# Dealing light expert groups at 0.92 instead of 0.86, and putting the routing weights behind the routing sort

## The chip, the cores and the metric

The kernel runs on one core of a Trainium2 chip. The metric is the device time of one execution in microseconds (us). Before the change it is 2007.69 us, the median of 3 runs (2006.3 to 2009.74).

## The reference

The program is a stack of two blocks over 256 tokens of width 1024, in float32: two hybrid layers (a gated recurrence beside dilated attention, then an MLP), a pooling mixer with a SwiGLU, and an attention mixer followed by a mixture of experts. Only the last part is touched:

```python
def moe_ffn(x, router, w_gu, w_down):
    B, S, D = x.shape
    xt = x.reshape(B * S, D)
    logits = (xt @ router).astype(jnp.float32)
    top_v, top_i = lax.top_k(logits, TOP_K)
    w = jax.nn.softmax(top_v, axis=-1)
    combine = jnp.einsum('tk,tke->te', w, jax.nn.one_hot(top_i, N_EXPERTS, dtype=jnp.float32)).astype(x.dtype)
    y = jnp.zeros_like(xt)
    for e in range(N_EXPERTS):
        y = y + combine[:, e:e + 1] * swiglu(xt, w_gu[e], w_down[e])
    return y.reshape(B, S, D)
```

Each expert has 1024 x 7168 gate and up weights and 3584 x 1024 down weights, so the eight experts read some 352 MB of weights, which is most of what the mixture does. A layer norm of `ALPHA * x + y` ends the program.

## The kernel before, in words

**Routing.** `Route.choose` ranks the logits of each token, `Route.place` counts the tokens of each expert, and `route_order` (L1193 on) sorts the experts by their count, heaviest first, with one-hot matrices on VectorE (DVE): `sort` (L1210 to L1214) multiplies the one-hot matrix `ge` with a column of `Q` and sums. Column 0 gives the experts' numbers, which are written to `ri` (L1218), from which the SP queue reads which expert's weights to load. Columns 2 and 3 give each token's slot, from which `select` (L1279) makes the matrices `P` that gather the tokens. Column 1 and `ov` (L1222 to L1224) say whether an expert has more tokens than the kernel's sizes allow, which leads to a branch at the end (L1635). Lines 1225 to 1246 make the weights of the choice: the two logits of each token, a softmax of two, and its sorted form `cw`. The program's scheduler orders the instructions of each engine; `high_priority` moves the sorts of columns 0, 2 and 3 to the front, and `behind(K, [i])` issues what is in it after instruction `i`.

**Experts.** The experts in sorted order are `E[0]` to `E[7]`. `E[0]` has two tiles of tokens (128 and 64 rows), `E[1]` to `E[3]` one of 128, `E[4]` and `E[5]` one of 64, `E[6]` and `E[7]` one of 32. Each expert is cut into 7 steps f of 512 hidden columns, and each step into 3 groups: gate (`up1`), up (`up2`) and down. A group reads 2 MB of weights in two blocks of 1 MB (`wload`, L132, tile `raw`, 7 buffers). `run_experts` is a generator that yields once a group.

- A group of `E[0]` to `E[3]` is split: ScalarE (ACT) rounds a block to `whi` (L147), DVE writes the rest to `wlo` (L148; 4 buffers of each), and TensorE (PE) multiplies three times (L209 to L211), 24 matmuls of 512 columns a group for a tile of 128 tokens. These experts are called heavy here.
- A group of `E[4]` to `E[7]` is not split: PE reads `raw` itself (L1340). The order lists 8 such matmuls a group, and the trace has two records for each. These experts are called light.

In `moe_layer` the heavy generator runs, and after each of its groups a number `due` grows; as many light groups as `due` says are dealt out between the heavy ones, in the order `E[6], E[7], E[4], E[5]`. What is left over comes after the heavy experts. The last down step of the last heavy expert is `finish`, which loads its weights in smaller parts. The sums over an expert's down steps stay in PSUM, for the second tile of `E[0]` in `sacc`; `weigh` (L1497, L1498) scales the sum of an expert by its weights, and `combine` (L1511 to L1513) adds it to `y`. After the branch at L1635 comes the layer norm (L283 to L291) and the store.

```python
            light, done, due = go([E[6], E[7], E[4], E[5]]), 0, 0.0
            for e, f in go(E[:4], hook, True):
                if E[6].tiles[0].xg is not None:
                    due += 0.86 if e.p else 1.5
                while done < int(due) and next(light, None):
                    done += 1
            for _ in light:
                pass
```

Of the kernel before, what the change touches and what calls it, by code (L numbers as in the profile page):

```python
# [13 lines left out]
AF = mybir.ActivationFunctionType  # L14
OP = mybir.AluOpType
AX = mybir.AxisListType
# [96 lines left out]
def wide(pool, n, size, dt=F32, **kw):  # L113


    return pool.tile([128, size // 4], dt, **kw)[:, :n]


def bc(ap, n):

    return ap[..., None].to_broadcast(list(ap.shape) + [n])
# [30 lines left out]
def behind(K, hold=None):  # L152

    es = ExitStack()
    for ins in K.hold if hold is None else hold:
        es.enter_context(K.tc.issue_after(ins.ins))
    return es
# [56 lines left out]
def bank(K, tag):  # L214
    return K.ps.tile([128, 512], F32, name=tag, tag=tag, bufs=K.banks[tag])
# [974 lines left out]
def route_order(K, pool, S):  # L1190


    nc = K.nc  # L1193
    sc, Q, lg, cst = S.sc, S.Q, S.lg, S.cst
    cnt = Q[:, 1, :]
    ca = cnt[:, :, None].to_broadcast([128, 8, 8])
    cb = cnt[:, None, :].to_broadcast([128, 8, 8])
    gt, ge = sc(8, 8), sc(8, 8)
    nc.vector.tensor_tensor(gt, cb, ca, op=OP.is_gt)
    nc.vector.tensor_tensor(ge, cb, ca, op=OP.is_equal)  # L1200
    nc.vector.tensor_tensor(ge, ge, cst("tri").rearrange("p (a b) -> p a b", a=8), op=OP.mult)
    nc.vector.tensor_tensor(gt, gt, ge, op=OP.add)
    pos = sc(8)
    nc.vector.tensor_reduce(pos, gt, axis=AX.X, op=OP.add)
    nc.vector.tensor_tensor(ge, pos[:, None, :].to_broadcast([128, 8, 8]),
                            cst("i8p").rearrange("p (a b) -> p a b", a=8), op=OP.is_equal)
    R = wide(pool, 48, 192 + 64, name="R").rearrange("p (a b) -> p a b", a=6)
    ri = pool.tile([1, 17], I32, name="ri")

    def sort(*qs):  # L1210
        for q in qs:
            g = sc(8, 8)
            nc.vector.tensor_tensor(g, ge, Q[:, q:q + 1, :].to_broadcast([128, 8, 8]), op=OP.mult)
            nc.vector.tensor_reduce(R[:, q, :], g, axis=AX.X, op=OP.add)  # L1214

    with K.tc.high_priority():
        sort(0)
        nc.vector.tensor_copy(ri[:, 0:8], R[0:1, 0, :])  # L1218
        sort(2, 3)
    sort(1)  # L1220
    ov = sc(9)[0:1]
    nc.vector.tensor_tensor(ov[:, 0:8], R[0:1, 1, :], cst("lim")[0:1, :], op=OP.is_gt)  # L1222
    nc.vector.tensor_reduce(ov[:, 8:9], ov[:, 0:8], axis=AX.X, op=OP.max)
    nc.vector.tensor_copy(ri[:, 16:17], ov[:, 8:9])  # L1224
    f = sc(2, 2, 8)
    for r in range(2):
        nc.vector.tensor_scalar(f[:, r], S.rk, float(r), None, op0=OP.is_equal)
    top = sc(2, 2, 8)
    sm = sc(6, 2)
    for r in range(2):  # L1230
        nc.vector.tensor_tensor(top[:, r], f[:, r], lg, op=OP.mult)
        nc.vector.tensor_reduce(sm[:, r, :], top[:, r], axis=AX.X, op=OP.add)
    nc.vector.tensor_tensor(sm[:, 2, :], sm[:, 1, :], sm[:, 0, :], op=OP.subtract)
    nc.scalar.activation(sm[:, 2, :], sm[:, 2, :], AF.Exp)
    nc.vector.tensor_scalar(sm[:, 3, :], sm[:, 2, :], 1.0, None, op0=OP.add)
    nc.vector.reciprocal(sm[:, 3, :], sm[:, 3, :])
    nc.vector.tensor_tensor(sm[:, 4, :], sm[:, 2, :], sm[:, 3, :], op=OP.mult)

    nc.vector.tensor_tensor(Q[:, 4:6, :], f[:, 0], bc(sm[:, 3, :], 8), op=OP.mult)
    nc.vector.tensor_tensor(top[:, 0], f[:, 1], bc(sm[:, 4, :], 8), op=OP.mult)  # L1240
    nc.vector.tensor_tensor(Q[:, 4:6, :], Q[:, 4:6, :], top[:, 0], op=OP.add)
    sort(4, 5)
    cw = pool.tile([128, 8, 2, 2], F32R, name="cw")
    for t in range(2):
        nc.vector.tensor_copy(cw[:, :, t, 0], R[:, 4 + t, :])
        nc.vector.tensor_tensor(cw[:, :, t, 1], R[:, 4 + t, :], cw[:, :, t, 0].bitcast(F32), op=OP.subtract)
    return R, ri, cw
# [315 lines left out]
def moe_layer(K, x, A, out, ps1, S):  # L1563
    nc = K.nc
    with ExitStack() as es:
# [6 lines left out]
        with K.tc.tile_pool(name="exp", reuse_waits="tile", bufs=1) as ep:  # L1572
            ps1.close()
            K.ps = es.enter_context(K.tc.tile_pool(name="psx", reuse_waits="tile", bufs=1,
                                                   space=bass.MemoryType.PSUM))
            K.banks = {"mm": 4, "acc": 4}
            K.iota = S.cst("iota")
            E = [Expert(p, t) for p, t in enumerate(([F0, H(128)], [F0], [F0], [F0], [(0, "s")], [(0, "s")], [(0, "q")],
                                                     [(0, "q")]))]
            with behind(K, [K.beat(5, S.last)]):  # L1580
                K.beat(14, S.place(1))
            R, ri, cw = route_order(K, pool, S)
            nc.vector.tensor_copy(K.identr, K.ident)
            K.iota = K.xp.tile([128, 256], F32, name="iota", tag="junk")[:, :128]
            nc.vector.tensor_copy(K.iota, S.cst("iota"))
            y = K.xTp.tile([128, 2, D], F32, name="y", tag="xT0")
            ye = K.xTp.tile([128, 2, D], F32R, name="ye", tag="xT1")
            K.ye, K.weighed = (ye[:, 0], ye[:, 1]), None
            for t in range(2):
                nc.vector.tensor_scalar(y[:, t, :], x[:, t, :], ALPHA, None, op0=OP.mult)  # L1590
            go = lambda *a: run_experts(K, ep, A, x, R, ri, cw, y, *a)
            E[0].tiles[1].sb = True
            b = [ep.tile([128, 2048], t, name=f"box{n}") for n, t in enumerate((F32R, F32, F32))]
            K.boxes["xg1"] = [b[0][:, 0:1024].rearrange("p (k o m) -> p k o m", o=1, m=128)]
            K.boxes["hT1"] = [b[0][:, c:c + 512].rearrange("p (k o m) -> p k o m", o=1, m=128) for c in (1024, 1536)]
            K.boxes["sg1"], K.boxes["sacc"] = [b[1][:, c:c + 512] for c in (0, 512)], [b[1][:, 1024:2048]]
            K.boxes["sgl"] = [b[2][:, c:c + 512] for c in (1024, 1536)]
            few_xg = b[2][:, 0:1024].rearrange("p (k m) -> p k m", m=128), ep.tile([128, KT, 64], F32, name="xgq")

            def few(xg, *ps):  # L1600

                w = xg.shape[2]
                P = ep.tile([128, 2, 128], F32, name="PL")[:, :, :w]
                for c, p in enumerate(ps):
                    tl = E[p].tiles[0]
                    o = slice(c * tl.m, (c + 1) * tl.m)
                    select(K, ep, R, p, tl)
                    for t in range(2):
                        nc.vector.tensor_copy(P[:, t, o], tl.P[:, t, :tl.m])
                    gather_w(K, ep, cw, p, tl, f"l{p}")  # L1610
                    tl.xg = xg[:, :, o]
                for k0 in range(0, KT, 4):
                    g = bank(K, "mm")[:, :4 * w].rearrange("p (a b) -> p a b", a=4)
                    for k in range(k0, k0 + 4):
                        for t in range(2):
                            nc.tensor.matmul(g[:, k % 4, :], x[:, t, k * 128:(k + 1) * 128], P[:, t, :],
                                             start=t == 0, stop=t == 1)
                    nc.scalar.activation(xg[:, k0:k0 + 4, :], g, AF.Copy)

            def hook(i):  # L1620
                if i == 0:
                    few(few_xg[1], 6, 7)
                if i == 2:
                    few(few_xg[0], 4, 5)

            light, done, due = go([E[6], E[7], E[4], E[5]]), 0, 0.0
            for e, f in go(E[:4], hook, True):
                if E[6].tiles[0].xg is not None:
                    due += 0.86 if e.p else 1.5
                while done < int(due) and next(light, None):  # L1630
                    done += 1
            for _ in light:
                pass
            over = nc.values_load(ri[0:1, 16:17], min_val=0, max_val=1)
            with K.tc.If(over > 0):  # L1635
                K.line = []
                rest = ((0, H(192)), (1, F1), (2, F1), (4, H(64)), (5, H(64)), (6, H(32)), (7, H(32)))
                for _ in go([Expert(p, [t]) for p, t in rest]):
                    pass
        with K.tc.tile_pool(name="fin", reuse_waits="tile", bufs=1) as fp:  # L1640
            g = row_bc(K, fp, A["ln_g_2"][1, 1], D, "lng")
# [123 lines left out]
```

## Time and profile before

| what | value |
|---|---|
| median of 3 runs | 2007.69 us (2006.3 to 2009.74) |
| the profiled execution, its own time | 2002.88 us |
| its span, first to last instruction | 2001.1 us |
| granted TensorE clock, mean | 0.989 |
| PE busy | 97% of the span |
| DVE busy | 63% |
| ACT busy | 48% |
| HBM read | 520.73 MB |

The span is the time between the first and the last instruction that the profile shows; 1.8 us of the execution lie around it. The profiled execution is 4.8 us below the median of the runs. The mixture of experts takes the stretch from about 1082 to 1987 us of the span. In the views, an engine's busy time is the union of its instructions' times; PEld is TensorE's loading of stationary operands, which runs beside its matmuls. An entry in square brackets is the idle time of that engine just before the row, with what ended it.

### The profile page before, as it was taken

The page shows a single profiled execution, that of the slowest core. Times are in us where ns is not written, and L with a number is a line of the kernel's source. Part 1 is how long each engine was busy: PE and PEld are TensorE (multiplying, and loading weights), DVE is VectorE, ACT ScalarE, POOL GpSimd, SP SyncE. Part 2 cuts the span into 40 slices and gives each one's busy share as a digit, 9 for nine tenths or more (in the row PEclk, how much of TensorE's full clock was granted, in tenths as well). Part 3 has the DMA queues.
Part 4 walks back from the last instruction along what each step waited for, and adds up shares of the span by engine and source line. Part 5 has one row for each costly group of instructions (what it writes and reads, how often), then busy time and mean ns, then how long its engine had stood idle before and what let it go on. Part 6 is the DMA issues. An engine that isn't in the chain of part 4 may idle for free. (4 is left out here: it accounts for less than half of the span.)

```text
span 2001.1 us, 27902 instructions
## 1 busy us (share of the span) xinstructions
PE 1934.3 (97%) x11066; PEld 1488.1 (74%) x11066; DVE 1263.4 (63%) x1723; ACT 960.8 (48%) x1197; POOL 33.5 (2%) x39
## 2 busy tenths in 40 slices
PE   7999999999999899999999999999999999999996
PEld 7879998887999899989877766666556655655563
DVE  6876555886556654466767655666765665656655
ACT  6565444665444433434343554445554554454442
POOL 0000000000000200000000000000000000000000
PEclk9999999999999999999998999999999999999998
DMA  9434554534555355551103989999999999999994
GB/s 345 164 115 158 180 191 168 183 129 169 194 185 189 137 202 188 173 195 53 48 1 144 371 365 381 389 400 368 426 427 419 403 397 417 405 406 380 419 419 167
DMA packets 137851, 523.68 MB, mean 262 GB/s; under 512 B 12016, under 2 KB 44144, under 8 KB 94832
## 3 DMA queue, kind: packets, MB, share of 16 engines
q1 hardware_dynamic: 137568, 521.74, 67.4%
q8 instruction: 89, 1.46, 0.3%
q14 instruction: 50, 0.41, 0.1%
q10 hardware_dynamic: 144, 0.07, 0.0%
HBM read 520.73 MB, written 1.05 MB: 261 GB/s over the span
## 5 line engine op out<-in xcount | busy, mean ns | idle before, releaser
L148 DVE TENSOR_TENSOR wlo<-raw,whi 128x2048 fp32r<-128x2048 f32 (+2 forms) x335 | 715.7, 2155 | 318.3 <-ACT whi L147 310.1
L147 ACT ACTIVATE whi<-raw 128x2048 fp32r<-128x2048 f32 (+2 forms) x337 | 600.2, 1805 | 307.3 <-issue 69.3
L209 PE MATMUL mm<-xT,whi 128*128 128x256 f32 (+1 forms) x824 | 237.2, 288 | 0.8 <-ACT mqk L459 0.4
L211 PE MATMUL mm<-xT,wlo 128*128 128x256 f32 (+1 forms) x824 | 234.4, 284 | 0.0
L210 PE MATMUL mm<-xT,whi 128*128 128x256 f32 (+1 forms) x824 | 233.9, 284 | 0.3
L210 PE MATMUL acc<-wlo,hT 128*128 128x512 f32 x568 | 224.5, 395 | 5.4 <-DVE wlo L148 5.4
L211 PE MATMUL acc<-whi,hT 128*128 128x512 f32 x568 | 221.6, 391 | 0.0
L209 PE MATMUL acc<-whi,hT 128*128 128x512 f32 x568 | 216.0, 394 | 3.5 <-ACT whi L147 3.5
L209 PE MATMUL mm<-whi,xg 128*128 128x512 f32 x448 | 181.6, 405 | 4.9 <-ACT whi L147 3.2
L210 PE MATMUL mm<-wlo,xg 128*128 128x512 f32 x448 | 179.5, 401 | 4.2 <-DVE wlo L148 4.2
L211 PE MATMUL mm<-whi,xg 128*128 128x512 f32 x448 | 176.5, 394 | 0.0
L209 PEld LDWEIGHTS mm<-xT,whi 128*128 128x128 f32 (+1 forms) x824 | 156.0, 189 | 4.6 <-issue 1.1
L210 PEld LDWEIGHTS mm<-xT,whi 128*128 128x128 f32 (+1 forms) x824 | 156.0, 189 | 3.3 <-DVE xT L678 1.1
L211 PEld LDWEIGHTS mm<-xT,wlo 128*128 128x128 f32 (+1 forms) x824 | 155.9, 189 | 0.6
L210 PEld LDWEIGHTS acc<-wlo,hT 128*128 128x128 f32 x568 | 106.7, 188 | 41.2 <-DVE wlo L148 8.8
L209 PEld LDWEIGHTS acc<-whi,hT 128*128 128x128 f32 x568 | 105.9, 188 | 34.4 <-issue 8.3
L211 PEld LDWEIGHTS acc<-whi,hT 128*128 128x128 f32 x568 | 106.6, 188 | 23.5 <-issue 1.7
L209 PEld LDWEIGHTS mm<-whi,xg 128*128 128x128 f32 x448 | 84.4, 188 | 47.0 <-issue 18.8
L210 PE MATMUL mx<-xT,whi 128*128 128x256 f32 x416 | 117.7, 283 | 0.0
L211 PE MATMUL mx<-xT,wlo 128*128 128x256 f32 x416 | 117.7, 283 | 0.0
L209 PE MATMUL mx<-xT,whi 128*128 128x256 f32 x416 | 117.7, 283 | 0.0
L210 PEld LDWEIGHTS mm<-wlo,xg 128*128 128x128 f32 x448 | 84.6, 189 | 36.9 <-issue 12.3
(381 smaller groups left out, 2902.3 us busy)
## 6 DMA issues: line engine op xcount, KB each, us to landing
raw<-in_moe_gu_dram SPq DMA_DIRECT2D x224, 1024.0 KB, 9.0
raw<-in_moe_dn_dram SPq DMA_DIRECT2D x110, 1024.0 KB, 8.6
raw<-in_w_up_dram SPq DMA_DIRECT2D x32, 1024.0 KB, 5.3
raw<-in_w_down_dram SPq DMA_DIRECT2D x32, 1024.0 KB, 5.1
raw<-in_w_in_dram SPq DMA_DIRECT2D x26, 1024.0 KB, 6.0
raw<-in_ffn_w_gu_dram SPq DMA_DIRECT2D x22, 1024.0 KB, 5.0
raw<-in_ffn_w_down_dram SPq DMA_DIRECT2D x11, 1024.0 KB, 4.7
raw<-in_nsa_w_in_dram SPq DMA_DIRECT2D x10, 1024.0 KB, 4.9
```

Source lines behind the costliest of these rows:

```text
L147: nc.scalar.activation(h, d, AF.Copy)
L148: K.lo.tensor_tensor(l, d, h.bitcast(F32), op=OP.subtract)
L209: nc.tensor.matmul(ps, l[0], r[0], start=start, stop=False)
L210: nc.tensor.matmul(ps, l[0], r[1], start=False, stop=False)
L211: nc.tensor.matmul(ps, l[1], r[0], start=False, stop=stop)
```

## The change

Two things change. The constant by which light groups are dealt behind the groups of `E[1]` to `E[3]` goes from 0.86 to 0.92. And everything in `route_order` that comes after the sort of columns 0, 2 and 3, which is the check for too many tokens and the weights of the choice, is put under `behind(K, [slots])`, where `slots` is the last reduction of the sort of column 3.

```diff
-            nc.vector.tensor_reduce(R[:, q, :], g, axis=AX.X, op=OP.add)
+            last = nc.vector.tensor_reduce(R[:, q, :], g, axis=AX.X, op=OP.add)
+        return last
...
-        sort(2, 3)
-    sort(1)
-    ov = sc(9)[0:1]
...
-    f = sc(2, 2, 8)
...
-    nc.scalar.activation(sm[:, 2, :], sm[:, 2, :], AF.Exp)
...
-    sort(4, 5)
+        slots = sort(2, 3)
+    with behind(K, [slots]):
+        sort(1)
+        ov = sc(9)[0:1]
...
+        f = sc(2, 2, 8)
...
+        nc.scalar.activation(sm[:, 2, :], sm[:, 2, :], AF.Exp)
...
+        sort(4, 5)
...
-                    due += 0.86 if e.p else 1.5
+                    due += 0.92 if e.p else 1.5
```

The new program's line numbers are two higher behind the first part. The order of DVE in the sort, before (L1227 to L1241 are the weights of the choice, L1199 to L1218 the sort up to `ri`, L1279 the gather matrices):

```order
L1200 TENSOR_TENSOR route<-route 128x64
L1233 TENSOR_TENSOR route<-route 128x2
L1201 TENSOR_TENSOR route<-route 128x64
L1202 TENSOR_TENSOR route<-route 128x64
L1235 TENSOR_SCALAR route<-route 128x2
...
L1213 TENSOR_TENSOR route<-route 128x64 x4
L1240 TENSOR_TENSOR route<-route 128x16
L1214 TENSOR_REDUCE R<-route 128x8 x4
L1241 TENSOR_TENSOR route<-route 128x16
L1218 CAST ri<-R 1x8
L1279 TENSOR_SCALAR P<-iota,R 128x128 x4
```

The same place in the changed program:

```order
L1201 TENSOR_TENSOR route<-route 128x64
L1202 TENSOR_TENSOR route<-route 128x64
L1204 TENSOR_REDUCE route<-route 128x8
L1205 TENSOR_TENSOR route<-route 128x64
L1213 TENSOR_TENSOR route<-route 128x64 x3
L1214 TENSOR_REDUCE R<-route 128x8 x3
L1213 TENSOR_TENSOR route<-route 128x64
L1219 CAST ri<-R 1x8
L1229 TENSOR_SCALAR route<-route 128x16 x2
L1281 TENSOR_SCALAR P<-iota,R 128x128 x3
L1214 TENSOR_REDUCE R<-route 128x8
L1281 TENSOR_SCALAR P<-iota,R 128x128
```

The weights' instructions have left the sort; two of them (L1229) now stand between `ri` and the gather matrices, and the others behind.

The end of DVE's order before the branch, before the change, in which `hT` is the transposed operand of the last heavy step, 128x1024 and 128x512 are the parts of `finish`, and the second L1498 with its L1513 belongs to the last light expert:

```order
L225 TENSOR_TENSOR hT_15516<-mm,hT_15516 128x4x128
L148 TENSOR_TENSOR wlo<-raw,whi 128x2048
...
L1439 COPY hTl<-mm 128x256
L148 TENSOR_TENSOR wlo<-raw,whi 128x1024 x2
L148 TENSOR_TENSOR wlo<-raw,whi 128x512 x4
L1498 SCALAR_TENSOR_TENSOR ye<-acc,cs,ye 128x512 x2
L1513 TENSOR_TENSOR y<-mm,y 128x512 x4
L1498 SCALAR_TENSOR_TENSOR ye<-acc,cs,ye 128x512 x2
L1513 TENSOR_TENSOR y<-mm,y 128x512 x4
```

The same place in the changed program, from the product of the last heavy gate and up (`sg`) on:

```order
L1429 TENSOR_TENSOR sg_15439<-mm,sg_15439 128x512
L148 TENSOR_TENSOR wlo<-raw,whi 128x2048
L1500 SCALAR_TENSOR_TENSOR ye<-acc,cs,ye 128x512
L148 TENSOR_TENSOR wlo<-raw,whi 128x2048
L1500 SCALAR_TENSOR_TENSOR ye<-acc,cs,ye 128x512
...
L148 TENSOR_TENSOR wlo<-raw,whi 128x1024 x2
L225 TENSOR_TENSOR hT_15567<-mm,hT_15567 128x4x128
L148 TENSOR_TENSOR wlo<-raw,whi 128x512 x4
L1500 SCALAR_TENSOR_TENSOR ye<-acc,cs,ye 128x512
L1515 TENSOR_TENSOR y<-mm,y 128x512
L1500 SCALAR_TENSOR_TENSOR ye<-acc,cs,ye 128x512
L1515 TENSOR_TENSOR y<-mm,y 128x512 x3
```

The last light expert's L1500 and L1515 now stand ahead of the parts of `finish`, among the last whole blocks, and the heavy expert's own stand last; `hT` stands behind four whole blocks and the two parts of 1024 columns.

## Rows read from the trace of the kernel before

**Rows 1.** Busy time of each engine by stretch: mixture by stages, then one saturated stretch

```profile
core 0: us, PE busy (x) PEld busy (x) DVE busy (x) ACT busy (x) POOL busy (x), PEclk, DMA share, GB/s
1342.00:1522.00 180.00, 170.65 (x860) 107.67 (x859) 125.09 (x109) 96.09 (x86) 0.00 (x0) 0.99 0.99 410
1522.00:1942.00 420.00, 416.50 (x1837) 248.47 (x1838) 258.75 (x191) 206.54 (x165) 0.00 (x0) 1.00 0.99 406
...
1402.00:1422.00 20.00, 19.92 (x107) 11.90 (x105) 14.74 (x15) 9.83 (x13) 0.00 (x0) 1.00 1.01 426
```

**Rows 2.** Who waited for whom: SP's queue from 1082 us, PE from 1342 to 1522

```profile
SPq L132 <- PE mm L1340: 260.4, 76, 10.9
...
PE acc L209 <- ACT whi L147: 2.9, 2, 2.1
PE mm L210 <- DVE wlo L148: 2.3, 2, 1.8
PE acc L210 <- DVE wlo L148: 2.2, 2, 1.4
```

**Rows 3.** PE in order of time: heavy matmuls, then a run of light ones

```profile
1936.40 0.39 PE L211 MATMUL mm<-whi,xg 128*128 128x512 f32 x1
...
1940.48 0.39 PE L211 MATMUL mm<-whi,xg 128*128 128x512 f32 x1
1940.80 1.94 PE L1340 MATMUL mm<-raw,box 128*64 128x512 f32 x8
1942.67 0.50 PE L209 MATMUL mm<-whi,xg 128*128 128x512 f32 x1
```

**Rows 4.** Groups by line and shape in the mixture (1082 to 1990 us), PE and DVE

```profile
L1340 PE MATMUL mm<-raw,xgq 128*32 128x512 f32 x448 | 56.4, 601 | 0.4 <-DMA raw<-in_moe_gu_dram 0.4
L1340 PE MATMUL acc<-raw,hTl 128*32 128x512 f32 x224 | 29.4, 604 | 0.0
L148 DVE TENSOR_TENSOR wlo<-raw,whi 128x2048 fp32r<-128x2048 f32 x166 | 377.1, 2285 | 108.2 <-ACT whi L147 100.3 <-PE mm L1332 7.0
```

**Rows 5.** Busy time of the light matmuls (L1340) alone, from 1522 to 1942

```profile
1522.00:1942.00 420.00, 140.72 (x606) 36.41 (x608) 1.00 0.99 406
```

**Rows 6.** DVE and SP's queue in order of time: the sort

```profile
1079.55 0.62 DVE L1213 TENSOR_TENSOR route<-route 128x64 f32<-128x64 f32 x4
1080.10 0.17 DVE L1240 TENSOR_TENSOR route<-route 128x16 f32<-128x16 f32 x1
1080.18 0.59 DVE L1214 TENSOR_REDUCE R<-route 128x8 f32<-128x64 f32 x4
1080.69 0.16 DVE L1241 TENSOR_TENSOR route<-route 128x16 f32<-128x16 f32 x1
1080.77 0.15 DVE L1218 CAST ri<-R 1x8 int32<-1x8 f32 x1
...
1082.03 18.11 SPq L132 DMA_DIRECT2D raw<-in_moe_gu_dram  x11
```

**Rows 7.** PE in order of time: the first heavy matmul

```profile
1088.93 0.50 PE L209 MATMUL mm<-whi,xg 128*128 128x512 f32 x1 [2.14 <-ACT whi L147]
```

**Rows 8.** The end, in order of time: PE, then ACT, then DVE

```profile
1954.65 0.73 PE L209 MATMUL acc<-whi,hT 128*128 128x512 f32 x2 [0.62 <-ACT whi L147]
1956.98 0.50 PE L210 MATMUL acc<-wlo,hT 128*128 128x512 f32 x1 [1.59 <-DVE wlo L148]
...
1979.90 1.94 PE L1340 MATMUL acc<-raw,hTl 128*64 128x512 f32 x8
...
1952.20 0.60 ACT L224 ACTIVATE hT<-mm 128x512 fp32r<-128x512 f32 x1 [4.05 <-PE acc L211]
...
1976.09 0.69 ACT L1497 ACTIVATE ye<-acc,cs 128x512 fp32r<-128x512 f32 x1 [1.80 <-PE acc L211]
...
1976.81 0.75 DVE L1498 SCALAR_TENSOR_TENSOR ye<-acc,cs,ye 128x512 fp32r<-128x512 f32 x1 [1.74 <-ACT ye L1497]
...
1983.94 2.58 DVE L1513 TENSOR_TENSOR y<-mm,y 128x512 f32<-128x512 f32 x4
```

More of the change, by code (lines that the diff above doesn't have):

```diff
@@ L1218, in route_order @@
         nc.vector.tensor_copy(ri[:, 0:8], R[0:1, 0, :])
-        sort(2, 3)
-    sort(1)
-    ov = sc(9)[0:1]
-    nc.vector.tensor_tensor(ov[:, 0:8], R[0:1, 1, :], cst("lim")[0:1, :], op=OP.is_gt)
-    nc.vector.tensor_reduce(ov[:, 8:9], ov[:, 0:8], axis=AX.X, op=OP.max)
-    nc.vector.tensor_copy(ri[:, 16:17], ov[:, 8:9])
-    f = sc(2, 2, 8)
[L1226 to L1232, printed above, removed]
@@ L1233, in route_order @@
-    nc.vector.tensor_tensor(sm[:, 2, :], sm[:, 1, :], sm[:, 0, :], op=OP.subtract)
-    nc.scalar.activation(sm[:, 2, :], sm[:, 2, :], AF.Exp)
[L1235 to L1240, printed above, removed]
@@ L1241, in route_order @@
-    nc.vector.tensor_tensor(Q[:, 4:6, :], Q[:, 4:6, :], top[:, 0], op=OP.add)
-    sort(4, 5)
+        slots = sort(2, 3)
+    with behind(K, [slots]):
+        sort(1)
+        ov = sc(9)[0:1]
+        nc.vector.tensor_tensor(ov[:, 0:8], R[0:1, 1, :], cst("lim")[0:1, :], op=OP.is_gt)
+        nc.vector.tensor_reduce(ov[:, 8:9], ov[:, 0:8], axis=AX.X, op=OP.max)
+        nc.vector.tensor_copy(ri[:, 16:17], ov[:, 8:9])
+        f = sc(2, 2, 8)
+        for r in range(2):
+            nc.vector.tensor_scalar(f[:, r], S.rk, float(r), None, op0=OP.is_equal)
+        top = sc(2, 2, 8)
+        sm = sc(6, 2)
+        for r in range(2):
+            nc.vector.tensor_tensor(top[:, r], f[:, r], lg, op=OP.mult)
+            nc.vector.tensor_reduce(sm[:, r, :], top[:, r], axis=AX.X, op=OP.add)
+        nc.vector.tensor_tensor(sm[:, 2, :], sm[:, 1, :], sm[:, 0, :], op=OP.subtract)
+        nc.scalar.activation(sm[:, 2, :], sm[:, 2, :], AF.Exp)
+        nc.vector.tensor_scalar(sm[:, 3, :], sm[:, 2, :], 1.0, None, op0=OP.add)
+        nc.vector.reciprocal(sm[:, 3, :], sm[:, 3, :])
+        nc.vector.tensor_tensor(sm[:, 4, :], sm[:, 2, :], sm[:, 3, :], op=OP.mult)
+        nc.vector.tensor_tensor(Q[:, 4:6, :], f[:, 0], bc(sm[:, 3, :], 8), op=OP.mult)
+        nc.vector.tensor_tensor(top[:, 0], f[:, 1], bc(sm[:, 4, :], 8), op=OP.mult)
+        nc.vector.tensor_tensor(Q[:, 4:6, :], Q[:, 4:6, :], top[:, 0], op=OP.add)
+        sort(4, 5)
```

## The prediction

> **What bounds the kernel now.** I read the busy time by stretch first. The sort and the start of the experts lie at 1070 to 1090 us, and the constant acts on everything after the first heavy expert, so these are the places. From 1342 to 1522 us, where the light experts with 32 tokens stand beside `E[1]`, PE is idle for 180 - 170.65 = 9.35 us, and the transfers run at up to 426 GB/s; from 1522 to 1942, with the light experts of 64 tokens, PE is idle for only 3.5 us in 420, and the transfers fall to 406 [rows 1]. Second, the waits: SP's queue waited 260.4 us for light matmuls to free a `raw` buffer [rows 2], so over much of the mixture the transfers follow PE and not the other way round. Third, PE in order of time: heavy matmuls start every (1940.48 - 1936.40)/18 = 0.227 us without a gap [rows 3]. So the first stretch is bound by transfers, the second by PE; a light group dealt earlier costs nothing in the second, something in the first, and changes what is left for the end. Last, the end [rows 8]: after PE's last light matmuls there is a chain of ACT, DVE, PE and DVE up to the last addition to `y`, and then the branch and the layer norm, which the change does not touch.
>
> **Prices of a group.** A heavy group of 24 matmuls takes 24 x 0.227 = 5.44 us of PE; with its share of the transposes (four in three groups, an estimate of 0.22 us from the matmuls' interval, of which the full 4 x 0.227/3 would be 0.3) 5.66. The light groups from 1522 to 1942 have 606 records [rows 5], 16 a group, so 37.9 groups, which at 0.86 stand beside 44.0 heavy ones; PE's 416.5 busy us less 44.0 x 5.66 leave 4.4 us for a light group of 64 tokens with all that goes with it, of which 140.72/37.9 = 3.7 are its matmuls, and 0.7 are around them. A light group of 32 tokens has (56.4 + 29.4)/42 = 2.0 us of matmuls [rows 4]; with the same 0.7 it takes 2.7. The transfer of a group is 2.1 MB, at 426 GB/s 4.92 us [rows 1].
>
> **Part 1, the sort.** On DVE the weights' instructions stand in the gaps of a dependent chain, so most of them cost the sort nothing. What does not fit: L1240 starts at 1080.10 and the reductions at 1080.18; L1241 takes 1080.69 to 1080.77, where `ri` is written [rows 6]. That is 0.08 + 0.08; the fourth reduction now stands behind `ri`, another 0.14 (a quarter of 0.59). I take 0.3 us, between 0 and 0.5, by which the first transfer (1082.03) starts earlier. The gather matrices gain less, as two small instructions stand ahead of them now. The weights themselves come later, some twenty small instructions behind the gather matrices, at 0.62/4 = 0.155 us each [rows 6] about 3 us. The first users of `cw` are matmuls that sit in front of the first heavy one on PE; PE is idle there for 2.14 us until ACT has split the first block [rows 7], and this idle time is what hides it. If all 3 us reached PE, 3 - 2.14 = 0.9 would be left, and nothing hides that; I put +1 us into the range for it. Part 1: **-0.3** (-0.5 to +1).
>
> **Part 2, the constant: how many groups stand where.** The heavy generator yields 83 times (28 + 28 + 27, the last down being `finish`). The first comes before the tokens of `E[6]` are gathered; 20 then count 1.5 for `E[0]`, that is 30 light groups; 62 follow. Before: 30 + 62 x 0.86 = 83.3, so 83 of 84 light groups are dealt, and the last one and the last light expert's sum come behind the heavy expert's end. After: 54/0.92 = 58.7, so all 84 are dealt by the 59th of the 62, and three heavy groups and `finish` stand alone at the end. There are 12 groups of 32 tokens left after `E[0]`; they take 14 heavy groups before and 13 after.
>
> *The stretch with 32 tokens.* Before, PE needs 14 x 5.66 + 12 x 2.7 = 111.6 us, the transfers 26 x 4.92 = 127.9: 16.3 us of a gap, of which 9.35 were seen as idle time, since the buffers were full at its start. After: 13 x 5.66 + 32.4 = 106.0 against 25 x 4.92 = 123.0, a gap of 17.0. That is **+0.7**.
>
> *The stretch with 64 tokens.* For each heavy group PE needs 5.66 + 0.86 x 4.4 = 9.44 us and the transfers 1.86 x 4.92 = 9.15; at 0.92 they are 9.71 and 9.45. PE stays the longer one, by 0.26 instead of 0.29. **0**; but the scheduler has written this stretch in a new order, and the idle time there is 3.5 us, so -3.5 to +3.5.
>
> *The end.* The light work that stood behind the heavy expert's end has gone ahead of it, as cover, at the same price on PE. What is left is the chain after PE's last accumulation. Before, it goes from 1979.90 + 1.94 = 1981.84 to 1983.94 + 2.58 = 1986.52: 4.7 us, for both halves of the light expert's columns at once [rows 8]. After, it is the second half of the heavy expert alone: ACT 0.69, DVE 0.75, three matmul starts and one end, 3 x 0.227 + 0.5, and two additions at 2.58/4 = 0.645, together 3.9, less what overlaps of the first matmuls, about 3.3. **-1.4** (-1.4 to 0).
>
> *Waits near the end.* Before, PE waits 0.62 and 1.59 us from 1954 to 1957 for a split block, because ACT stood for 4.05 us before `hT` with the split behind it on its queue [rows 8]. With other work there I take this stall to go: -2.2. What is late next is DVE. From `sg` to the last `hT` its order now holds four whole blocks at 2.285 [rows 4], two scalings of 0.75, four additions of 0.645 [rows 8], two parts of half a block's columns, 2.285 together, and `hT`, as long as an addition: 16.2 us. It begins with `sg`, about as long, and so some 0.9 after PE. PE has in the same place one light run of 1.87 [rows 3], 48 heavy matmuls (10.9), eight of `combine` (1.8) and four transposes (0.9 at most): 15.5. 16.2 + 0.9 - 15.5 leave PE a wait of 1.6 us, in pieces; I take 1.8 with the first blocks: **-2.2 + 1.8 = -0.4** (-2.2 to +4).
>
> The sum is -0.3 + 0.7 + 0 - 1.4 - 0.4 = **-1.4 us**. Against the profiled execution, 2002.88, that is 2001.5; that execution is 4.8 us below the median of the runs, so against 2007.69 it is **2006.3 us**. 0.2% is 4.0 us, about what a measurement of this kernel can tell from no change, and the forecast lies inside.
>
> **The rivals.**
> *Slower: the heavy groups that stand alone wait for DVE.* A heavy group is two blocks; DVE splits them in 4.57 us and has `sg`, `hT` and, here, the last light expert's scalings and additions beside them. Over the last three groups it is as full as PE, by the sum above, and where PE waited for a block in the first stretch it waited 7.4/6 = 1.2 us each time [rows 2]. If PE waits so at each of the six blocks, and again at `finish`, whose two parts stand ahead of `hT` on DVE, that is 7 x 1.2 = 8.4 us in place of 1.8: -1.4 + 6.6 = +5.2, **2012.9 us**. It decides as soon as DVE's work from `sg` to `hT` is over 2 us longer than PE's. For it: no light work is left to fill PE's gaps there. Against: in the stretch with 64 tokens DVE is busy 259 of 420 us and PE hardly waits. On this bears a rule of the Trainium skill (Perfetto Trace Analysis, Optimization Strategy): regimes with different limits gain by being interleaved. It speaks against this change, which takes three heavy groups out of the mix; the rows so far show mixed stretches only. 0.16.
>
> *The transfers are the bound in the second stretch too.* If 406 GB/s is all that they give there, a group costs 5.17 us of transfer, whatever PE does. Before: 26 x 4.92 + 90 x 5.17 = 593.2; after: 25 x 4.92 + 88 x 5.17 + 3 x 5.66 = 595.0. That is +1.8 in place of +0.7, a sum of -0.3: **2007.4 us**. The 3.5 us of idle time on PE speak against it [rows 1]. The Trainium skill (Perfetto Trace Analysis, Identifying the Most-Contended Engine) has TensorE judged by its weight loads and not by the busy matmuls: 248 of 420 us are 59%, far from full, and by it the transfers would be the bound. 0.12.
>
> *Faster: the new order takes waits out of the first stretch as well.* If half of PE's 7.4 us of waits there go, and DVE's 1.8 at the end don't come, the sum is -1.4 - 3.7 - 1.8 = -6.9: **2000.8 us**. For it: each of these waits is one block that came late behind something on ACT or DVE, and such an order is written anew. Against: a gap of transfers stands behind them, which grows. 0.25.
>
> *The change does nothing to the bound part*: the scheduler puts the light work where it was, and only part 1 acts: **2007.4 us**. The rows of the end in the new order speak against it. 0.05.
>
> **How the numbers follow.** The forecast has 0.42. Faster by over 0.2%: the faster rival, 0.25, and a good end of the forecast's ranges (-3.5 in the second stretch), 0.06: 0.31. Slower: the slower rival, 0.16, and 0.03 of the forecast: 0.19. Within: 0.50. The range is 1999.5 to 2012.5 us, which takes in most of the faster rival and the near side of the slower one.
>
> **What would show it.** After: `ri` 0.3 us earlier in DVE's rows; PE's idle time some 0.7 us more in the first stretch and about the same in the second; no light matmul behind the heavy expert's last ones; 3.3 us from PE's last accumulation to the last addition to `y`; PE waits of about 1.8 us in the last 20 us before that. It is wrong if PE waits over 4 us for splits at the end, or if idle time in either stretch moves by more than 4 us.

## The result, and the profile after

The changed kernel takes 2029.4 us (median of 4 runs, 2027.99 to 2030.44), the kernel before, on the same chip, 2008.11 (4 runs, 2006.3 to 2009.74). The ratio is 1.0107, with a 95% interval of 1.0094 to 1.0119: slower by 21 us, outside the predicted range of 1999.5 to 2012.5. The profiled execution takes 2029.24 us, with a span of 2027.4 and a mean granted clock of 0.985 (before 0.989).

Busy time by stretch of the kernel after: the start of the mixture, and the two stretches of before (behind a row's length: PE, PEld, DVE, ACT, POOL, then granted clock, DMA share, GB/s):

```profile
1082.00:1172.00 90.00, 84.97 (x475) 64.36 (x474) 58.80 (x103) 48.82 (x57) 0.00 (x0) 0.94 0.88 361
1342.00:1522.00 180.00, 167.08 (x833) 103.51 (x834) 118.05 (x105) 90.08 (x84) 0.00 (x0) 0.97 0.97 400
1522.00:1942.00 420.00, 410.69 (x1792) 239.42 (x1788) 251.74 (x190) 197.87 (x159) 0.00 (x0) 1.00 0.98 397
```

PE is idle for 12.9 us from 1342 to 1522 (before 9.35) and for 9.3 from 1522 to 1942 (before 3.5 [rows 1]). The transfers have become slower, 397 for 406 GB/s, which fits transfers that follow PE. The granted clock is lower as well, in the second row (0.97 for 0.99) and in the first, where the profile of before has 1.00:

```profile
1082.00:1172.00 90.00, 85.31 (x509) 64.44 (x508) 58.66 (x93) 50.06 (x59) 0.00 (x0) 1.00 0.93 382
```

Who PE waited for in the kernel after, from 1082 to 2015 us (us in total, times, longest):

```profile
PE mm L210 <- DVE wlo L148: 10.1, 6, 1.9
PE acc L210 <- DVE wlo L148: 7.8, 7, 2.5
PE mm L209 <- ACT whi L147: 5.7, 5, 1.7
PE acc L209 <- ACT whi L147: 2.1, 1, 2.1
PE mm L1513 <- DVE y L1515: 1.9, 2, 1.5
PE mm L209 <- DVE fu L1348: 1.2, 1, 1.2
PE mm L1321 <- DVE cw L1248: 1.0, 2, 0.5
```

Most of it is waiting for split blocks: 25.7 us in the first four rows. In the kernel before, from 1082 to 1995 us, the same four sum to 16.3:

```profile
PE acc L210 <- DVE wlo L148: 5.4, 6, 1.6
PE mm L210 <- DVE wlo L148: 4.2, 5, 1.8
PE acc L209 <- ACT whi L147: 3.5, 3, 2.1
PE mm L209 <- ACT whi L147: 3.2, 2, 2.1
```

All PE waits in the mixture are 32.7 us for 20.6.

**One such place.** PE and then ACT of the kernel after, in order of time:

```profile
1474.66 1.92 PE L1342 MATMUL mm<-raw,xgq 128*32 128x512 f32 x16
1478.24 0.50 PE L209 MATMUL mm<-whi,xg 128*128 128x512 f32 x1 [1.66 <-ACT whi L147]
1480.57 0.50 PE L210 MATMUL mm<-wlo,xg 128*128 128x512 f32 x1 [1.82 <-DVE wlo L148]
```

```profile
1475.79 0.59 ACT L1347 ACTIVATE box<-mm 64x512 f32<-64x512 f32 x1 [11.19 <-PE mm L1342]
1476.29 1.90 ACT L147 ACTIVATE whi<-raw 128x2048 fp32r<-128x2048 f32 x1
```

A light group (L1342) is the last thing on PE before the next heavy one. On ACT the copy that folds the light group's result (L1347) stands ahead of the split of the heavy block. ACT does nothing for 11.19 us until that light matmul has run; only then it copies, 0.59 us, and splits, 1.90 us, and then DVE makes `wlo`. PE has nothing else to run, and waits 1.66 and 1.82 us. The split did not wait for its transfer: by the semaphore that it waits for, its block had landed at 1468.82, 7 us before the copy could start.

The nearest such place of the kernel before, PE and then ACT:

```profile
1472.66 1.07 PE L1340 MATMUL mm<-raw,xgq 128*32 128x512 f32 x8
1473.66 0.50 PE L211 MATMUL mm<-whi,xg 128*128 128x512 f32 x1
1474.09 1.06 PE L1340 MATMUL mm<-raw,xgq 128*32 128x512 f32 x8
```

```profile
1466.64 1.92 ACT L147 ACTIVATE whi<-raw 128x2048 fp32r<-128x2048 f32 x1 [5.43 <-DMA raw<-in_moe_gu_dram]
1473.80 0.59 ACT L1345 ACTIVATE box<-mm 64x512 f32<-64x512 f32 x1 [5.24 <-PE mm L1340]
```

The same copy waits for the same kind of matmul, but a block was split ahead of it, at 1466.64, and the light matmuls lie between heavy ones. PE goes on without a gap up to 1478.7, where it waits 0.49 us for the next `wlo`. So the wait does not come from a longer instruction, but from which of two instructions stands first in a queue. The Trainium skill (PSUM — Partial Sum Buffer, Engine vs sequencer instructions) says that the queues of ScalarE and VectorE are strictly first in, first out; the trace agrees: for the last 7 of the 11.19 us a block that had landed stood behind the copy.

DVE has the same form of it, three times in the first stretch; the longest, DVE and the PE row that waits for it:

```profile
1434.72 0.69 DVE L1429 TENSOR_TENSOR sg<-mm,sg 128x512 f32<-128x512 f32 x1 [1.64 <-PE mm L211]
1435.33 2.28 DVE L148 TENSOR_TENSOR wlo<-raw,whi 128x2048 fp32r<-128x2048 f32 x1
```

```profile
1437.67 0.79 PE L210 MATMUL acc<-wlo,hT 128*128 128x512 f32 x1 [2.53 <-DVE wlo L148]
```

DVE stands for 1.64 us for the heavy step's own product `sg`, with the split behind it.

**The clock.** Behind such waits the granted clock falls. The two rows behind the pair at 1478 and 1480 (columns as above):

```profile
1480.00:1482.00 2.00, 1.43 (x6) 1.22 (x7) 2.00 (x3) 1.64 (x3) 0.00 (x0) 0.99 0.86 311
1482.00:1484.00 2.00, 2.00 (x6) 1.51 (x6) 1.71 (x2) 1.57 (x1) 0.00 (x0) 0.50 0.93 373
```

At 0.50, which is 1.2 GHz, a heavy matmul starts every 0.43 us instead of 0.227. I count (1 - granted clock) x time over rows of 2 us as time lost to the clock. That is 13.7 us after: 5.1 at 1088 to 1100, and 1.7 each at 1368, 1437, 1482, 1571 and 1977. At 1368 and 1437 it follows single waits of 2.10 and 2.53 us, at the last three places pairs. In the profile of before it is 1.7, at 1364. The Trainium skill (TensorE: Matmul & The Clock Gate, HAM oscillation) tells of a matmul kernel that pays for a wait twice, once idle and once in slower matmuls behind it; the two rows agree.

**The start and the end.** DVE of the kernel before at its copy of the last counts from PE (L1186), then DVE and SP's queue, then PE, of the kernel after:

```profile
1077.80 0.17 DVE L1186 COPY route<-acc 128x8 f32<-128x8 f32 x1
```

```profile
1078.08 0.17 DVE L1186 COPY route<-acc 128x8 f32<-128x8 f32 x1
1080.64 0.15 DVE L1219 CAST ri<-R 1x8 int32<-1x8 f32 x1
1081.90 12.12 SPq L132 DMA_DIRECT2D raw<-in_moe_gu_dram  x9
```

```profile
1086.25 0.27 PE L1321 MATMUL mm<-cw,Pr 128*128 128x2 f32 x1 [0.55 <-DVE cw L1248]
1086.93 0.27 PE L1321 MATMUL mm<-cw,Pr 128*128 128x2 f32 x1 [0.41 <-DVE cw L1248]
1088.73 0.50 PE L209 MATMUL mm<-whi,xg 128*128 128x512 f32 x1 [1.52 <-ACT whi L147]
```

`ri` is written 0.13 us earlier and the first transfer starts 0.13 earlier (1082.03 before [rows 6]). These are times in two executions, whose start moves: the unchanged kernel's second profile, e12 below, has `ri` at 1079.59. Counted from L1186, `ri` follows after 2.97 us before and after 2.56 in the changed kernel. All the profiles below with the old sort have 2.96 or 2.97, and e2, the only other one with the new sort, has 2.56; so the sort itself is 0.41 us shorter. The weights now reach PE late, by 0.55 and 0.41 us, inside the time in which PE waits for the first block anyway; the first heavy matmul starts at 1088.73 for 1088.93 [rows 7].

PE near the end, then DVE's last additions before the branch:

```profile
1964.89 0.50 PE L210 MATMUL mm<-wlo,xg 128*128 128x512 f32 x1 [1.87 <-DVE wlo L148]
...
1975.02 0.50 PE L209 MATMUL mm<-whi,xg 128*128 128x512 f32 x1 [0.62 <-ACT whi L147]
1977.35 0.79 PE L210 MATMUL mm<-wlo,xg 128*128 128x512 f32 x1 [1.83 <-DVE wlo L148]
...
2003.46 0.50 PE L211 MATMUL acc<-whi,hT 128*128 128x512 f32 x1 [0.62 <-DVE hT L225]
```

```profile
2010.52 1.97 DVE L1515 TENSOR_TENSOR y<-mm,y 128x512 f32<-128x512 f32 x3
```

The last light matmuls start at 1986.29, well ahead of the heavy expert's end, as the count of groups had it. PE's last accumulation ends at 2008.54, the last addition to `y` at 2012.49: 3.95 us later (before 4.7 [rows 8]). Between the light work and that accumulation PE waits once, 0.62 us. The pair of waits 0.62 and 1.59, which stood at a down step before [rows 8], has a like one at a gate or up group, 0.62 and 1.83, and now the clock falls with it. The wait of 1.87 us at 1964.89 is new.

### The profile page after: what moved, and what is told of

Same layout as the page of the kernel before. It is cut to its first block, busy times and chain, and to the rows that moved or that the text cites. A ratio compares the mean times of both kernels' runs of the same rounds, so it can differ in the third digit from the quotient of the medians.

```text
span 2027.4 us, 27893 instructions
## 1 busy us (share of the span) xinstructions
PE 1947.2 (96%) x11066; PEld 1493.3 (74%) x11066; DVE 1264.0 (62%) x1723; ACT 958.7 (47%) x1197; POOL 33.6 (2%) x39
## 5 line engine op out<-in xcount | busy, mean ns | idle before, releaser
L209 PE MATMUL mm<-whi,xg 128*128 128x512 f32 x448 | 185.0, 413 | 7.0 <-ACT whi L147 5.7
L211 PE MATMUL mm<-whi,xg 128*128 128x512 f32 x448 | 178.6, 399 | 0.0
L209 PEld LDWEIGHTS acc<-whi,hT 128*128 128x128 f32 x568 | 106.2, 188 | 32.7 <-issue 8.3
L210 PEld LDWEIGHTS mm<-wlo,xg 128*128 128x128 f32 x448 | 86.1, 192 | 46.0 <-DVE wlo L148 14.7
```

What stands on the lines that cost most here:

```text
L209: nc.tensor.matmul(ps, l[0], r[0], start=start, stop=False)
L210: nc.tensor.matmul(ps, l[0], r[1], start=False, stop=False)
L211: nc.tensor.matmul(ps, l[1], r[0], start=False, stop=stop)
```

## The experiments

My theory (A) is that the new order puts light work ahead of splits, so that PE waits, and that the clock falls behind the waits. Its rivals are the sort and the start of the mixture, the number 0.92 itself as a rate (C), and, in the last runs, losses of single stretches that add up (D). All changes are made to the kernel before unless said otherwise. In each profile three numbers are read: PE's waits in the mixture, the time lost to the clock, and when the last addition to `y` ends. The last column is that end less the two others.

| run | us, median | ratio to before, 95% | PE waits | clock | last `y` | rest |
|---|---|---|---|---|---|---|
| before | 2008.11 | | 20.6 | 1.7 | 1986.5 | 1964.2 |
| after | 2029.4 | 1.0107 (1.0094 to 1.0119) | 32.7 | 13.7 | 2012.5 | 1966.1 |
| e1 0.92 alone | 2031.23 | 1.0114 (1.0095 to 1.0133) | 34.1 | 17.0 | 2018.1 | 1967.0 |
| e2 sort alone | 2010.52 | 1.0012 (1.0000 to 1.0025) | 22.4 | 6.8 | 1994.0 | 1964.8 |
| e3 0.89 | 2019.88 | 1.0063 (1.0045 to 1.0081) | 27.8 | 13.7 | 2001.3 | 1959.8 |
| e4 0.83 | 2022.01 | 1.0072 (1.0055 to 1.0090) | 28.7 | 13.6 | 2003.1 | 1960.8 |
| e5 0.86, `due` from 0.5 | 2022.34 | 1.0078 (1.0057 to 1.0100) | 27.3 | 15.3 | 2007.0 | 1964.4 |
| e15 0.86, `due` from 0.25 | 2012.34 | 1.0021 (1.0011 to 1.0031) | 22.9 | 3.4 | 1992.0 | 1965.7 |
| e13 0.92, `due` from 0.5 | 2023.34 | 1.0074 (1.0056 to 1.0093) | 29.0 | 15.3 | 2010.6 | 1966.3 |
| e14 0.92, `due` from 0.25 | 2031.96 | 1.0117 (1.0095 to 1.0139) | 32.7 | 17.1 | 2016.6 | 1966.8 |
| e11 0.92 behind `E[1]` only | 2021.75 | 1.0077 (1.0060 to 1.0094) | 29.4 | 10.2 | 2003.7 | 1964.1 |
| e16 0.92 behind `E[2]`, `E[3]` only | 2008.63 | 1.0002 (0.9993 to 1.0012) | 21.6 | 8.6 | 1994.0 | 1963.8 |
| e7 0.92, pin | 2028.73 | 1.0107 (1.0086 to 1.0127) | 33.0 | 15.4 | 2013.1 | 1964.7 |
| e8 0.86, pin | 2008.12 | 1.0004 (0.9994 to 1.0013) | 20.8 | 5.1 | 1992.2 | 1966.3 |
| e9 0.92, folds later | 2022.68 | 1.0080 (1.0064 to 1.0097) | 29.3 | 10.2 | 2006.0 | 1966.5 |
| e10 0.86, folds later | 2016.14 | 1.0040 (1.0027 to 1.0052) | 24.7 | 13.7 | 2000.5 | 1962.1 |
| e6 filled gap | 2006.08 | 0.9988 (0.9979 to 0.9998) | 19.1 | 6.8 | 1991.1 | 1965.2 |
| e12 before, unchanged | 2009.81 | 1.0012 (1.0002 to 1.0023) | 22.2 | 8.5 | 1992.0 | 1961.3 |

The rest stays within 1960 to 1967 us in all eighteen profiles, whatever the order. So the differences between the kernels are PE's waits and the clock, to some 3.5 us either way, and to 7 at most between any two. Part of that spread lies ahead of the mixture: the first heavy matmul starts at 1086.0 to 1091.5 us, and from it to PE's last matmul before the branch the rest is 875.2 to 879.9. The light and heavy matmuls themselves cost much the same everywhere. And e12, which is the kernel before run once more, reads 0.12% above it: ratios within about that are not told from no change.

**Which part.** e1 is the constant alone, e2 the sort alone (the changed kernel with 0.86).

```diff
-                    due += 0.86 if e.p else 1.5
+                    due += 0.92 if e.p else 1.5
```

> The kernel before with 0.92 alone. Theory A (a new order puts splits of heavy blocks behind blocked rows on ACT's queue; PE waits, and its clock falls after the longest waits): most of the +21 us, +15 to +22, with the first heavy step at the time of before, since the clock's fall at 1090 us belongs to the sort. Theory B (the sort's later weights cost the time, and the constant none): within 4 us of before.

> The changed kernel with 0.86 back, so only the sort's part. Theory A: the fall of PE's clock behind the first gather stays, first heavy step about 4.4 us later than before, and +3 to +6 us in all, unless the slightly new order behind it takes or gives waits. Theory B: +15 to +22 us.

The constant alone loses all of it, 23 us; the sort alone reads +2.4, the ratio that the unchanged kernel has in e12. The sort is not the cause. The fall of the clock at the start, which had been put down to the sort, came the other way round: e1, with the old sort, has it (5.1 us), and e2 has none there.

**The number or the places.** e3 and e4 set 0.89 and 0.83 in the same line. e5 keeps 0.86 and moves every dealing by half a group; e15 by a quarter; e13 and e14 do the same at 0.92.

```diff
-            light, done, due = go([E[6], E[7], E[4], E[5]]), 0, 0.0
+            light, done, due = go([E[6], E[7], E[4], E[5]]), 0, 0.5
```

> The kernel before with 0.89. If the number of light groups dealt early sets the cost (theory C: more transfers early, PE short of work), half of what 0.92 costs, about +10 us. Theory A (the order that the scheduler happens to write): no fixed relation; anywhere from -5 to +20 us, and PE's waits for whi and wlo together with the clock's falls account for the difference within 4 us.

> The kernel before with 0.83: two more light groups are left for the end. Theory C: about -10 us by the early stretches, less what the end gains. Theory A: no fixed relation, and more likely slower, since the light groups left over stand alone at the end; PE's waits and clock falls account for the difference within 4 us.

> The kernel before with 0.86, but the count of light groups due starts at 0.5 instead of 0, so each heavy group has as many light ones beside it as before and only their places shift by half a group. Theory A (the order decides, not the number): 5 to 20 us slower than before, with PE's waits for splits and clock falls that account for it within 4 us. Theory C (the number of light groups dealt early decides): within 4 us of before.

> The kernel before with 0.92 and with due starting at 0.5 instead of 0. If the loss belongs to the places at which light work meets the splits (A), another phase of the same number gives another time, anywhere from 2008 to 2035, and the part by which it differs from the 2031.2 us of the constant alone is again the difference in PE waits and time at 1.2 GHz, within 3.5 us. If the loss belongs to the number 0.92 (C), it stays at 2031 +- 3.

> The kernel before with 0.92 and with due starting at 0.25. A: another time again, 2008 to 2035, different from that of the half shift. C: 2031 +- 3.

> The kernel before with 0.86 unchanged and with due starting at 0.25. A, with 0.86 in a good order by its places: slower than before, by about 10 us as with the half shift. C: within 0.2% of the kernel before.

0.83, below the old number, is as slow as 0.89 above it. But 0.83 does not lose its time at the splits: the waits for them are 15.8 us, no more than in the kernel before, and what is new are waits for DVE's additions to `y`, the largest of them

```profile
PE mm L1340 <- DVE y L1513: 4.9, 2, 2.9
```

So in e4 the order costs PE its time at another place than the splits. The half shift at 0.86 costs 14 us with no change of rate. At 0.86 the three starts give 2008.3, 2012.3 and 2022.3, at 0.92 2031.2, 2032.0 and 2023.3. So the places matter by 9 to 14 us at one and the same number, and C falls as the whole cause. A missed too: it gave e15 some 10 us, which cost 4, and it gave e14 a time of its own, which came out as that of e1. At each of the three starts 0.92 is the slower one, by 22.9, 19.6 and 1.0 us; that the higher number makes bad places likelier is not excluded by six kernels.

**Where.** e11 deals at 0.92 behind the groups of `E[1]` alone, e16 behind all others.

```diff
-                    due += 0.86 if e.p else 1.5
+                    due += (0.92 if e.p == 1 else 0.86) if e.p else 1.5
```

> The kernel before with 0.92 behind the groups of the second heavy expert only and 0.86 behind the others. In the trace of the constant alone, 14 of the 23 us are lost up to the eighteenth heavy step. Theory A with its place in the first stretch: +8 to +18 us. If the later stretch with 64-token groups costs most: under +6 us.

> 0.86 behind the groups of E[1], 0.92 behind those of E[2] and E[3]: the counterpart of 0.92 behind E[1] alone, which cost 13.4 us of the 23. If the losses of the stretches add up (D), this costs the other 10 us, 2018 +- 3. If each order is a new lot (A), it can be anything from 2008 to 2032.

e11 loses 13.4 us, e16 nothing, and both together, e1, 23: D falls. Up to 1580 us e11 has nearly the waits of the changed kernel, 2 to 5 us earlier. (Its later light groups move too: 21 groups of `E[1]` at 0.06 more leave `due` 1.26 higher from there on.) PE of e11 at the place shown above:

```profile
1475.19 0.50 PE L209 MATMUL mm<-whi,xg 128*128 128x512 f32 x1 [1.66 <-ACT whi L147]
1477.52 0.80 PE L210 MATMUL mm<-wlo,xg 128*128 128x512 f32 x1 [1.83 <-DVE wlo L148]
```

e16 keeps what before had. Its busy time from 1342 to 1522 and from 1522 to 1942:

```profile
1342.00:1522.00 180.00, 171.01 (x866) 106.74 (x862) 124.20 (x110) 97.45 (x88) 0.00 (x0) 0.99 0.99 411
1522.00:1942.00 420.00, 415.82 (x1831) 245.18 (x1831) 257.74 (x194) 203.40 (x163) 0.00 (x0) 1.00 0.99 407
```

PE is idle for 9.0 and 4.2 us, as before (9.35 and 3.5 [rows 1]), though light groups are dealt out at 0.92 through most of the second row. So what e1 loses behind `E[1]` is not the rate's own; I take it to hang on where the dealing of `E[1]` ends, which was not tried by itself.

**What stands ahead of the splits.** e7 and e8 tie the light fold's copy behind the last split that the program has written by then.

```diff
-            nc.scalar.activation(h, d, AF.Copy)
+            K.split = nc.scalar.activation(h, d, AF.Copy)
...
-    K.nc.scalar.activation(a, ps[64:128, :], AF.Copy)
+    with behind(K, [K.split]):
+        K.nc.scalar.activation(a, ps[64:128, :], AF.Copy)
```

> The kernel before with 0.92, and ACT's copy out of PSUM of a light group (L1345) is issued behind the last heavy split that the program has emitted, so a split no longer stands behind that copy. Theory A: PE's waits for whi and wlo fall from some 25 us to under 15 and the time from 2031 to 2010 to 2020 us. Theory C: no gain; 2025 to 2035 us. Rival to both (the copy then waits for the split's transfer and holds the light matmuls' bank): slower than 2035.

> The same pin with 0.86. Theory A: before has few such waits left to win, 13 us of waits for splits after 1342, so 0 to -8 us against before. Rival: slower by 5 us or more, since the copies wait for transfers.

Both are as without the tie. ACT of e7 at the place says why:

```profile
1475.25 0.59 ACT L1346 ACTIVATE box<-mm 64x512 f32<-64x512 f32 x1 [12.76 <-PE mm L1340]
1475.75 1.90 ACT L147 ACTIVATE whi<-raw 128x2048 fp32r<-128x2048 f32 x1
```

The copy still stands ahead of the split: the program writes that split after the copy, so the tie was to an earlier one. e7 and e8 say nothing on A. e9 and e10 therefore write the light copies, their silu and product after the next heavy group, with the tie as well:

```diff
+            if tl.full:
+                pend.append(lambda a=a, ps=ps, tl=tl: nc.scalar.activation(a[:tl.m], fold(K, pool, a[:64], ps, tl.m), AF.Silu))
+                continue
...
+    def flush():
+        for p in pend:
+            p()
+        pend.clear()
```

> The kernel before with 0.92, and the copy out of PSUM, the fold and the product of a light group are emitted only after the next heavy group with its next block's splits, and pinned behind these splits on ACT. Theory A (splits stand behind such copies on ACT, the copies wait for PE): PE's waits for whi and wlo fall from 26 us to under 15, its clock falls with them, and the time goes from 2031 to 2008 to 2020 us. Rival E (the splits are late for their transfer, the copy in front of them costs nothing): the waits stay above 22 us and the time within 2026 to 2036. Rival F (a light group now holds its bank longer, and PE waits for banks): slower than 2036 us.

> The same with 0.86. Theory A: 0 to -8 us against before, and the difference between 0.92 and 0.86 shrinks from 23 to under 10 us. Rival E: within 4 us of before. Rival F: 5 us slower or more.

Who PE waited for in e9, the largest rows:

```profile
PE mm L210 <- DVE wlo L148: 8.0, 7, 1.8
PE acc L1340 <- DMA raw<-in_moe_dn_dram: 5.5, 2, 5.0
PE acc L210 <- DVE wlo L148: 5.2, 6, 1.4
PE mm L209 <- ACT whi L147: 4.3, 3, 2.3
```

The waits for splits fall from 28.8 us in e1 to 17.5 (1.2 us of the fall lies at the start, where executions differ), and the time by 8.6. A had forecast under 15 us of them and a time of 2008 to 2020 us, and missed both by some 2.5. The fall of the waits and of the time fits waits that come from what stands ahead of the splits; it does not show this by itself, as the edit also writes a new order everywhere. It is no gain over before: one transfer, for which PE did not wait in e1, is waited for, 5.0 us, with a fall of the clock behind it, and SP's queue waits up to 13.0 us there for `wlo` to free a buffer (2.2 in e1). At 0.86, where little was to be had, only that price is seen (+7.8 us). 0.92 is 6.5 us slower than 0.86 in this form, and 23 in the old.

**The start.** The 5 us of clock at 1088 to 1100 are not the change's. e12, the kernel before unchanged, has them too: PE, and four us of it by window.

```profile
1087.65 0.50 PE L209 MATMUL mm<-whi,xg 128*128 128x512 f32 x1 [3.49 <-ACT whi L147]
```

```profile
1088.00:1092.00 4.00, 4.00 (x21) 4.00 (x20) 3.85 (x3) 2.44 (x3) 0.00 (x0) 0.51 1.01 426
```

> The kernel before, unchanged, for a second profile. Theory D (in most executions the clock falls behind the gap before the first heavy matmul): the profile shows a stretch at half clock between 1085 and 1100 us and a span 3 to 6 us above 2001. Rival (it does not fall in this kernel): clock full there and a span within 2 us of 2001, or longer for another cause.

In the profile shown ahead of the prediction PE waited 2.14 us there [rows 7] and kept 1.00. There the low clock came earlier, at 0.81 from 1080 to 1084, and took the matmuls ahead of the gather (L1124, 14 of them in 5.25 us for 3.45 in e12); the gather began later, at 1082.71 for 1079.98, and ran at 1.00. With the 5.1 us that e12 loses behind its wait, I take this to be why that execution lies 4.8 us below its median. It is a rare one: of 65 other executions of the kernel before on record, five have a mean granted clock of 0.989 or 0.990 as it has, and four of these took 2002.7 to 2003.2 us; the other sixty, at 0.985 to 0.988, have a median of 2008.4. e6 fills the gap with three matmuls whose product isn't used:

```diff
+            ps = bank(K, "acc")
+            with behind(K, [K.gw]), K.tc.high_priority():
+                for i in range(3):
+                    nc.tensor.matmul(ps, x[:, 0, 0:128], x[:, 0, 0:512], start=i == 0, stop=i == 2)
```

(`K.gw` is the gather's last `cw` matmul.)

> The kernel before with three matmuls of 512 columns on x between the first gather and the first heavy matmul, where PE stands idle; their product is not used. Theory D (the clock falls behind that idle time in most executions, which the profile of before did not show, and costs 4 to 5 us): median 3 to 5 us faster than before, near 2003 us, clock full from 1085 to 1100 us. Rival (the clock's fall there belongs to the changed kernels alone): median within 1 us of before, or up to 2 us slower by the added matmuls.

PE's wait becomes 0.61 us, and the clock stays at 1.00 up to 1106; then it falls all the same, for 3.4 us of loss where e12 has 6.8 up to 1116:

```profile
1089.09 0.50 PE L209 MATMUL mm<-whi,xg 128*128 128x512 f32 x1 [0.61 <-ACT whi L147]
```

```profile
1108.00:1110.00 2.00, 2.00 (x9) 1.81 (x9) 1.00 (x9) 1.01 (x2) 0.00 (x0) 0.50 1.01 426
```

At 0.9988 (0.9979 to 0.9998) it is the fastest kernel of the study, 2.3 us below the kernel before where 3 to 5 were expected; but its ratio is no further from 1 than that of e12, between equal kernels.

## Why the prediction was wrong

**Part 1, the sort: right.** -0.3 was forecast for `ri`; the sort is 0.41 us shorter. The weights reached PE late by 0.96 us in two pieces, all of it hidden by PE's wait for the first block, as the step had it.

**The stretch with 32 tokens: the wrong step.** "That is +0.7" came from sums of PE and transfer time. Its count is off: 13 x 0.92 is 11.96, so the twelfth light group falls due behind the 14th heavy one, as before, and by these sums nothing changes. Nor was the stretch bound as it had it: of PE's idle time there 8.4 of 9.35 us were waits for split blocks, and 10.8 of 12.9 after; 0.4 us was a wait for a transfer, and none after. Idle time rose by 3.6 us and the clock took another 3.4. The sum asked how much work there is, and not whether each heavy block is split in time. The faster rival held the right mechanism, "each of these waits is one block that came late behind something on ACT or DVE, and such an order is written anew", with one sign only: a new order was priced at a gain of 3.7 us and never at a loss, though the order on record had 9.35 us of idle time where others of these kernels have up to 14.6 (e13).

**The stretch with 64 tokens: the other wrong step.** "0; [...] so -3.5 to +3.5": the upper end was the idle time that was there, which bounds a gain, not a loss. Idle time rose by 5.8 us, and the text had named a move of more than 4 as what would make it wrong. e16 shows that the balance argued there was right: the higher rate itself costs nothing in that stretch. e11 shows that the waits at its start come from `E[1]`.

**The clock had no term.** Beside waits that grew by 12.1 us, 12.0 us more were lost at 1.2 GHz. About 5 of these the kernel before has as well, in e12, and they were missing from the execution profiled first; the other 7 follow the new waits. Against e12 the waits grew by 10.5 us and the loss at 1.2 GHz by 5.2. So the new waits cost about half as much again as they read.

**The end: right in kind, half its size.** The light work did go from behind the heavy expert, and the chain is 3.95 us where 3.3 was forecast and 4.7 was before: -0.7 for -1.4. The difference is a second wait for DVE's scaling, which stands behind the first addition.

**Waits near the end: wrong on what goes, nearer on what comes.** "I take this stall to go: -2.2": one of its form is there, 0.62 and 1.83 us, as ACT now stands for `sg` with the split behind it. With the 1.87 us at 1964.89 PE waits 4.3 us for splits from 1960 on, over the 4 that the prediction had named as wrong. DVE's load behind the light work cost 0.62 us; 1.8 was taken.

**The rivals.** The slower rival gave the right sign for another reason. It had PE wait for DVE once the heavy groups stand alone; there PE waits 0.62 us in all, and is busy for 14.7 of 15 us from 1988 to 2003. With that the rule of the Trainium skill on interleaving (Perfetto Trace Analysis, Optimization Strategy) is not borne out here: taking heavy groups out of the mix cost nothing that the trace shows. The transfers as the bound fall too: from 1522 to 1942 no wait of PE in the kernel after ended with a transfer, and e16 deals at 0.92 there with 407 GB/s and no loss. That the change does nothing to the bound part is refuted.

**What stays open.** Why one pair of waits brings the clock down and another, like 0.62 and 1.83 us at 1763 to 1766, with 1.00 behind it, does not. And whether 0.92 has a cost of its own behind `E[1]`: six kernels show that the places move the time by 9 to 14 us, not that the number has no share.

## What to carry to other kernels

When a number that deals out work changes, the scheduler writes a new order for all engines, and the sums of work say little: ask for each split or copy which instruction stands ahead of it in its queue, and what that one waits for. The idle time in the profile of before bounds what a new order can gain, not what it can lose, and each wait may be paid a second time in matmuls at 1.2 GHz. Before such a number is taken for a rate, time its neighbours on both sides and the same number from another start: here that shows an old setting that sat in a good order, and not on a slope.

## What was unexpected of the hardware

A stretch in which PE is busy for 93% (1342 to 1522) still loses its clock: two waits of 1.66 and 1.82 us with one matmul between them were followed by 0.50, at a price of 1.7 us, about as much as one of the waits. In eight of the profiles a wait of 3.2 to 3.6 us at the start is followed by 1.2 GHz for some 10 us of full work, 5 us of loss; filling it (e6) moved the fall to 1106 and did not remove it.
